# A decode step with a product-key expert layer: index tiles, the sample's gate block, the dot products and the sample's sums take other places

## The chip, the cores and the metric

The kernel runs on one core of a Trainium2 chip. The metric is the time of one execution on the device in microseconds; the times given are medians over several executions. One more execution was recorded by the hardware profiler, and all lines quoted from a profile or a trace come from such an execution. TensorE is PE in the profile (PEld its weight loads), VectorE is DVE, ScalarE is ACT, GpSimd is POOL, SyncE is SP.

## The reference, cut to what matters

The kernel computes one layer of a decoder for 256 prompt tokens and 32 sample tokens (8 sequences of 4). Attention, recurrence, output projection and the first normalisation come first and are not touched. What matters is the expert layer at the end and the normalisation behind it:

```python
def peer_ffn(x, wq, subkeys, u_tab, v_tab):            # x: (B, T, 2048)
    q = (xt @ wq).reshape(n, P_HEADS, 2, P_DKEY // 2)  # 8 heads, two halves of a key
    s = jnp.einsum('nhcd,hckd->nhck', q, subkeys)
    hv, hix = lax.top_k(s, P_TOPK)                     # 16 of 128 in each half
    cand = hv[:, :, 0, :, None] + hv[:, :, 1, None, :]
    cand_e = hix[:, :, 0, :, None] * N_KEYS + hix[:, :, 1, None, :]
    tv, tpos = lax.top_k(cand, P_TOPK)                 # 16 experts per head: 128 per token
    expert = jnp.take_along_axis(cand_e, tpos, axis=-1)
    gate = jax.nn.softmax(tv, axis=-1)
    def block(xb, eb, gb):
        h = jax.nn.gelu(jnp.einsum('cd,chkd->chk', xb, u_tab[eb]), approximate=False)
        return jnp.einsum('chk,chkd->cd', gb * h, v_tab[eb])

x = layer_norm(DEEPNORM_ALPHA * x + peer_ffn(x), ln2_g, ln2_b)
```

There are 128 x 128 = 16384 experts, each with a row of 2048 in `u_tab` and one in `v_tab`, all in float32.

## The kernel before, in words

**The expert layer of the prompt.** The expert number is written as i1 * 128 + i2. For the first 896 columns of x the kernel gathers, for each of the 128 chosen experts of a token, the row piece from a table in HBM and multiplies and sums it on VectorE: a *dot* (`dot`, L1795, one VectorE instruction of 128 tokens x 896 and a read of its sum; `fetch` and `gather`, L455, give it its rows through POOL and a ring `rows` of five buffers). There are 2 x 128 dots, one for each half of the prompt's tokens and each of the 128 choices. For the other 1152 columns it multiplies with every expert on PE: 128 *blocks* (`dense`, L1862 to L1869) of 128 experts each, whose weights come over SP into a ring `ur` of five buffers. The results of the blocks stand in `AW`.

The loop at L1872 writes a block and then one or two dots (`ND`, `NDN`), in seven of eight blocks two. Two dots come before the loop. The 14 dots left behind the loop are written into the first 12 steps of the picking (`NDL`).

**The table.** `table(t)` (L1800) forms for half t of the tokens what the picking reads, transposed: i1, i2, gate and dot of every choice. The two numbers are cut out of the expert number in the tile `ii` (a single buffer, two uses per call), and PE transposes them. `table(0)` is written once eight dots of the second half are done, `table(1)` at step 30.

**The picking.** 64 steps of four tokens each, run as a software pipeline in one loop of 68 (L1973). In a step, `pick` compares all positions with i1 and i2 on VectorE (tile `oo`, L1898), transposes one of them on PE and copies it on ACT; `picked` multiplies it with `AW` on PE (`px`); `product_of` multiplies with the other and sums on VectorE (L1921), adds the dot and takes the Gelu on ACT; `gated` multiplies with the gate; `scaled` scales the comparison on ACT; `put` multiplies both back into `AW` on PE (`pa`) and ACT copies them out.

**The sample's sums.** The 32 sample tokens have their activations already. Their rows of the second table are gathered (`smp_fetch`, two gathers of 512 KB on POOL, into the same ring `rows`) and summed on PE (`smp_add`, tile `fs`, four matmuls with a block `ws` as weights, which spreads each gate over its tokens). 32 such sums stand in steps 14 to 62. `ws` is formed on VectorE ahead of the loop (L1951). Behind the loop the sample's x is added, normalised (`norm_quarters`: statistics on VectorE, one small matmul on PE, a chain of small VectorE instructions, one ACT instruction, two more products) and written out by 16 DMAs on SP (L2013).

**The V stage.** 128 blocks of the second table, three columns groups on PE (L2067) with `AW` as weights, the rows over SP (`rows_load`, L1970), and the last 640 columns by gathers on POOL and sums on VectorE (`row_add`, L2040). The first rows are loaded early into a place of their own; those of the second and third block come in program order behind the sample's outputs on SP.

**What sets the order.** The instructions are written for a planner that puts each engine's queue in order by modelled durations: an instruction that looks ready may move ahead of earlier ones on its engine. Each engine then runs its queue strictly in that order. `pin` (`keep_in_program_order`) holds an instruction behind the one that was written just before it for the same engine. All instructions of the picking are pinned, and the dots inside it too (`keep=True`); the dots of the blocks, `ws`, `table` and the sample's norm are not. `issue_after` holds an instruction behind one that is named. The pools `up`, `dp`, `x4p` and `vp` are stacks on the left side of SBUF: `x4p` (with `ws`) lies where `dp` (with `ur`) was, and `vp` (V stage) lies where `up` and `x4p` were.

Of the kernel before, what the change touches and what calls it, by code (L numbers as in the profile page):

```python
# [12 lines left out]
I32 = mybir.dt.int32  # L13
U32 = mybir.dt.uint32
AF = mybir.ActivationFunctionType
OP = mybir.AluOpType
AX = mybir.AxisListType
PSUM = bass.MemoryType.PSUM
P = 128
# [5 lines left out]
ALPHA = 2.0 ** 0.25  # L25
# [23 lines left out]
NP1 = 8  # L49
NDW = 1  # L50
ND = 1
NDN = 7
NDL = 12
NUR = 5
NRW = 5
NDB = 9
# [94 lines left out]
def hybrid_decode_step(ctx: ExitStack, tc: tile.TileContext, a, outs, dbg=None):  # L151
    nc = tc.nc
    ve, sc, pe, gp, sy = nc.vector, nc.scalar, nc.tensor, nc.gpsimd, nc.sync
# [35 lines left out]
    def bank(tag="pb"):  # L189
        places = [(pool, nm, n) for _, div in psum for t_, pool, nm, n in div for _ in range(n) if t_ == tag]  # L190
        turn[tag] = k = (turn.get(tag, -1) + 1) % len(places)
        pool, nm, n = places[k]
        return pool.tile([P, 512], F32, name=tag, tag=nm, bufs=n)
# [58 lines left out]
    C0, ld = consts(cp, 0)  # L252
# [1536 lines left out]
    def dot(n=1, upto=2 * P, keep=False, ahead=NRW):  # L1789

        for i in range(got[1], min(got[1] + n, upto)):
            t, s_ = dots[i]
            fetch(min(i + ahead, upto))
            r_, h_ = rows_.pop(i), HD[t][:, s_:s_ + 1]
            i_ = ve.scalar_tensor_tensor(r_, r_, 1.0, X1a[t], op0=OP.mult, op1=OP.mult, accum_out=h_)  # L1795
            if keep:
                tc.keep_in_program_order(i_)
            got[1] = i + 1

    def table(t):  # L1800

        pb = bank("pb")
        for q, (op_, v_) in enumerate(((OP.logical_shift_right, 7), (OP.bitwise_and, 127))):
            ii = up([P, P], "ii", I32)
            iff = ii.bitcast(F32)
            ve.tensor_scalar(ii, GI[t], v_, None, op0=op_)
            ve.tensor_copy(iff, ii)
            pe.transpose(pb[:, 128 * q:128 * q + 128], iff, ident)
        pe.transpose(pb[:, 256:384], GE[t], ident)
        pe.transpose(pb[:, 384:], HD[t], ident)  # L1810
        sc.copy(TB[:, :, P * t:P * t + P], pb.rearrange("p (a b) -> p a b", a=4))
# [56 lines left out]
            mm = pe.matmul(ph[:, :NPR], w[:, e, :], Xfd[:, e, :], start=(e == 0), stop=(e == NDB - 1))  # L1868
        return mm, sc.copy(AW[:, i1 // 64, :, i1 % 64], ph[:, :NPR])  # L1869

    tabled = []
    for i1 in range(P):  # L1872
        mm, end = dense(i1)
        n_ = ND + (i1 * NDN % 8 < NDN)
        dot(min(max(P - got[1], 0) or n_, n_))
        if got[1] >= P + 8 and not tabled:
            with tc.issue_after(mm.ins), tc.issue_after(end.ins):
                table(0)
            tabled.append(0)
    kc.close()  # L1880
    dp.close()
    if not tabled:
        dot(P - got[1])
        table(0)
    x4p, vr = Pool("x4", "left"), Pool("vr", "right")
    ig, vh2 = [GI[2], IG], vtab.rearrange("n (q c) -> (n q) c", q=2)
    banks(pt=2, px=2, pa=2, pb=1, fs=1)
# [60 lines left out]

    x4p([P, 4, P], "oT", bufs=2)
    ws = x4p([P, 32, 32], "ws")  # L1950
    ve.tensor_tensor(ws, C0("sum4")[:, None, :32].to_broadcast([P, 32, 32]), GE[2][:, :, None].to_broadcast([P, 32, 32]), OP.mult)  # L1951
    fs, sr = bank("fs"), {}

    def smp_fetch(j):
# [5 lines left out]
    def smp_add(j):  # L1960
        for c in range(4):
            pin(pe.matmul(fs[32 * c:32 * c + 32, :], ws[:, j, :], sr[j, c // 2][:, 512 * (c % 2):512 * (c % 2) + 512],  # L1962
                          start=(j == 0), stop=(j == 31)))

    raw = {}

    def rows_load(k):

        raw[k] = (vp if k % 3 else vr)([P, FD], "v_", bufs=2 if k % 3 else 1)
        return sy.dma_start(raw[k], vtab[P * k:P * k + P, :FD])  # L1970

    left = 2 * P - got[1]
    for s_ in range(68):  # L1973
        if s_ == 30:
            table(1)
        oT = pick(s_) if s_ < 64 else None
        if 3 <= s_ < 66 and s_ % 2:
            gated(s_ // 2 - 1)
        if s_ >= 4:
            put(s_ - 4)  # L1980
        if 0 <= s_ - 3 < 64:
            scaled(s_ - 3)
        if oT is not None:
            picked(s_, oT)
        if 0 <= s_ - 1 < 64:
            product_of(s_ - 1)
        if s_ < NDL:
            dot(-(-left * (s_ + 1) // NDL) + 2 * P - left - got[1], keep=True)
        for j in range(32):
            if s_ == NDL + j * (62 - NDL) // 32:  # L1990
                smp_fetch(j)
        for j in range(32):
            if s_ == NDL + 2 + j * (62 - NDL) // 32:
                smp_add(j)
        if s_ == 46:
            bs_, gs_, x_ = (xa_[:, 512 * n:512 * n + 512] for n in range(3))
            for q in range(4):
                r_, c_ = slice(32 * q, 32 * q + 32), slice(512 * q, 512 * q + 512)
                sy.dma_start(x_[r_, :], X1D[NPR:NT, c_])
                for t_, nm in ((gs_, "ln2_g"), (bs_, "ln2_b")):  # L2000
                    sy.dma_start(t_[r_, :], bass.AP(tensor=a[nm].tensor, offset=a[nm].offset + 512 * q, ap=[[0, 32], [1, 512]]))
        if s_ == 50:
            rows_load(0)
    pb = bank("pb")
    for t in range(2):
        pe.transpose(pb[:, 128 * t:128 * t + 128], TB[:, 2, P * t:P * t + P], ident)
        sc.copy(GE[t], pb[:, 128 * t:128 * t + 128])

    ve.scalar_tensor_tensor(x_, x_, ALPHA, fs, op0=OP.mult, op1=OP.add)
    norm_quarters(x4p, x_, gs_, bs_, "pb")  # L2010
    for q in range(4):
        for i in range(4):
            sy.dma_start(outs[1][:, i, 512 * q:512 * q + 512], x_[32 * q + 8 * i:32 * q + 8 * i + 8, :])  # L2013
    x4p.close()
    up.close()
    banks(pj=2, pb=6)
# [136 lines left out]
```

## Time and profile before

| | |
|---|---|
| median of three executions | 2479.08 us (2474.55 to 2487.72) |
| the profiled execution's own time | 2475.65 us |
| its span in the trace | 2473.9 us |
| PE busy | 2255.7 us (91%) |
| VectorE busy | 1745.4 us (71%) |
| POOL busy | 1336.1 us (54%) |
| expert blocks on PE | 1187.8 to 1685.8 us |
| picking, first to last comparison | 1680.2 to 1916.9 us |
| V stage, first to last matmul | 1931.2 to 2451.4 us |

A line of the trace in order of time reads: start, duration, engine, source line, operation, what it writes and reads, its shape, and in brackets how long its engine stood idle before it and which instruction ended that. In a table of windows a stretch is followed by its length, the busy time of the engines with the number of instructions in brackets, the granted clock of PE, the share of the DMA engines' time in use, and the bytes moved in GB/s.

### The profile page before, as it was taken

The page shows a single profiled execution, that of the slowest core. Times are in us where ns is not written, and L with a number is a line of the kernel's source. Part 1 is how long each engine was busy: PE and PEld are TensorE (multiplying, and loading weights), DVE is VectorE, ACT ScalarE, POOL GpSimd, SP SyncE. Part 2 cuts the span into 40 slices and gives each one's busy share as a digit, 9 for nine tenths or more (in the row PEclk, how much of TensorE's full clock was granted, in tenths as well). Part 3 has the DMA queues.
Part 4 walks back from the last instruction along what each step waited for, and adds up shares of the span by engine and source line. Part 5 has one row for each costly group of instructions (what it writes and reads, how often), then busy time and mean ns, then how long its engine had stood idle before and what let it go on. Part 6 is the DMA issues. An engine that isn't in the chain of part 4 may idle for free.

```text
span 2473.9 us, 42694 instructions
## 1 busy us (share of the span) xinstructions
PE 2255.7 (91%) x15628; PEld 1886.1 (76%) x15628; DVE 1745.4 (71%) x3985; ACT 820.4 (33%) x1591; POOL 1336.1 (54%) x1419
## 2 busy tenths in 40 slices
PE   7979999997988997789999999995899799999996
PEld 7867898885645665578888888884777688888885
DVE  5789766555563446889856545556877799998888
ACT  3433222223341433220111111111777444443443
POOL 5678423233345005578666644655444588886672
PEclk9999999998896996899999999997999899999998
DMA  7777986449478984798699989995666699999994
GB/s 218 229 236 225 284 216 177 119 143 278 171 243 252 316 302 146 288 321 267 213 400 404 398 329 401 383 393 169 181 209 197 242 369 363 363 362 362 345 358 187
DMA packets 327602, 684.09 MB, mean 277 GB/s; under 512 B 82270, under 2 KB 200992, under 8 KB 326464
## 3 DMA queue, kind: packets, MB, share of 16 engines
q1 hardware_dynamic: 246176, 342.58, 41.7%
q0 software_dynamic: 81216, 338.78, 38.2%
q8 instruction: 123, 2.02, 0.3%
q14 instruction: 87, 0.71, 0.1%
HBM read 665.69 MB, written 23.88 MB: 279 GB/s over the span
## 4 chain that ended last, share of the span: by engine, by line
PE 46%; issue 14%; DVE 13%; POOL 11%; DMA 8%; ACT 2%; SPq 1%; POOLq 0%; DVEq 0%; ACTq 0%
PE pb L2067 19%; POOL rows L455 8%; PE pj L424 6%; PE pa L1661 3%; PE px L1910 2%; PE p L1081 2%; DVE sr L1557 2%; PE pa L1943 2%; DMA big<-in_state_rwkv 1%; PE ss L1498 1%; DMA co<-in_cache_cmp_kv,gidx 1%; PE pt L1902 1%; PE fs L1962 1%; DMA rows<-in_peer_u_g,gi 1%; DVE CA L478 1%
## 5 line engine op out<-in xcount | busy, mean ns | idle before, releaser
L1868 PE MATMUL ph<-Xfd,ur 128*128 128x256 f32 x2304 | 497.8, 379 | 0.0
L1868 PEld LDWEIGHTS ph<-Xfd,ur 128*128 128x128 f32 x2304 | 437.4, 190 | 59.5
L455 POOL DMA_INDIRECT rq<-in_peer_v_g,gi x256 | 378.5, 1479 | 142.0 <-DVE fP L2040 86.7
L455 POOL DMA_INDIRECT rows<-in_peer_u_g,gi x256 | 292.5, 1143 | 229.8 <-DVE rows L1795 199.5
L1795 DVE SCALAR_TENSOR_TENSOR rows<-rows,x1a 128x896 f32<-128x896 f32 x256 | 280.2, 1098 | 178.4 <-DMA rows<-in_peer_u_g,gi 178.0
L424 PE MATMUL pj<-XH,wl 128*128 128x288 f32 (+1 forms) x752 | 231.7, 308 | 14.9 <-DVE wl L419 8.5
L424 PE MATMUL pj<-XH,wh 128*128 128x288 f32 (+1 forms) x752 | 229.5, 305 | 15.2 <-DVE ss L754 6.9
L2040 DVE SCALAR_TENSOR_TENSOR fP<-rq,ge,fP 128x640 f32<-128x640 f32 x254 | 223.7, 881 | 5.7 <-DMA rq<-in_peer_v_g,gi 3.3
L424 PE MATMUL pj<-XL,wh 128*128 128x288 f32 (+1 forms) x752 | 225.9, 301 | 0.0
L2067 PE MATMUL pb<-vl,ah 128*128 128x512 f32 (+1 forms) x768 | 207.6, 378 | 1.3 <-DVE vl L2060 0.5
L1869 ACT COPY AW<-ph 128x256 f32<-128x256 f32 x128 | 77.2, 610 | 396.6 <-PE ph L1868 391.5
L2067 PE MATMUL pb<-vh,ah 128*128 128x512 f32 (+1 forms) x768 | 188.0, 380 | 22.1 <-ACT vh L2059 22.1
L2067 PE MATMUL pb<-vh,al 128*128 128x512 f32 (+1 forms) x768 | 205.8, 376 | 0.0
L417 ACT CAST wh<-wraw 128x512 fp32r<-128x512 f32 (+1 forms) x188 | 114.8, 616 | 228.9 <-PE pj L424 175.6
L2067 PEld LDWEIGHTS pb<-vh,ah 128*128 128x128 f32 x768 | 145.5, 196 | 44.9 <-ACT vh L2059 25.7
L478 DVE SCALAR_TENSOR_TENSOR CA<-co,wbc,CA 128x256 f32<-128x256 f32 x248 | 133.4, 575 | 48.7 <-DMA co<-in_cache_cmp_kv,gidx 48.7
L424 PEld LDWEIGHTS pj<-XH,wl 128*128 128x128 f32 (+1 forms) x752 | 143.8, 191 | 26.8 <-DVE wl L419 12.5
L2067 PEld LDWEIGHTS pb<-vl,ah 128*128 128x128 f32 x768 | 144.9, 195 | 24.2 <-DVE vl L2060 5.1
L424 PEld LDWEIGHTS pj<-XH,wh 128*128 128x128 f32 (+1 forms) x752 | 144.1, 192 | 21.4 <-DVE ss L754 7.3
L2067 PEld LDWEIGHTS pb<-vh,al 128*128 128x128 f32 x768 | 145.3, 195 | 19.4
L424 PEld LDWEIGHTS pj<-XL,wh 128*128 128x128 f32 (+1 forms) x752 | 144.2, 192 | 1.5 <-issue 1.2
L419 DVE TENSOR_TENSOR wl<-wraw,wh 128x512 fp32r<-128x512 f32 (+1 forms) x141 | 101.8, 731 | 44.4 <-ACT wh L417 43.8
(844 smaller groups left out, 4339.2 us busy)
## 6 DMA issues: line engine op xcount, KB each, us to landing
ur<-in_peer_u_t SPq DMA_DIRECT2D x128, 576.0 KB
wraw<-in_w_in SPq DMA_DIRECT2D x152, 256.0 KB
cw<-in_w_out SPq DMA_DIRECT2D x32, 512.0 KB
wraw<-in_w_out SPq DMA_DIRECT2D x32, 512.0 KB
wraw<-in_peer_wq SPq DMA_DIRECT2D x32, 512.0 KB
cw<-in_peer_wq SPq DMA_DIRECT2D x32, 512.0 KB
wraw<-in_w_in SPq DMA_DIRECT2D x64, 128.0 KB
co<-in_state_win_kv SPq DMA_DIRECT2D x16, 512.0 KB
```

Of the source, the lines that this page charges most:

```text
L417: sc.copy(wh[:, :, :n], w[:, :, :n])
L419: i_ = en.tensor_tensor(wl[:, :, :n], w[:, :, :n], wh[:, :, :n].bitcast(F32), OP.subtract)
L424: last[2] = pe.matmul(pb[:n, :nt], wi[:, k, :n], xi[(o + k) // 8][:, (o + k) % 8, :nt], start=(o + k == 0 and wi is wh and xi is xh), stop ...
L455: gp.indirect_dma_start(out=dst, out_offset=None, in_=rows_, in_offset=bass.IndirectOffsetOnAxis(ap=ix, axis=0))
L478: ve.scalar_tensor_tensor(d_, x_, w_, d_, op0=OP.mult, op1=OP.add)
L1081: pe.matmul(pb[hs[c], 64 * m:64 * m + 64], lhs(hs[c], m), rhs(hs[c], m), start=True, stop=True)
L1661: pe.matmul(acc[t], xi[:, e, P * t:P * t + P], wi[:, e, :], start=(k == e == n_ == 0), stop=(k == 6 and e == 1 and n_ == 2))
L1795: i_ = ve.scalar_tensor_tensor(r_, r_, 1.0, X1a[t], op0=OP.mult, op1=OP.mult, accum_out=h_)
L1868: mm = pe.matmul(ph[:, :NPR], w[:, e, :], Xfd[:, e, :], start=(e == 0), stop=(e == NDB - 1))
L1869: return mm, sc.copy(AW[:, i1 // 64, :, i1 % 64], ph[:, :NPR])
L2040: ve.scalar_tensor_tensor(fP[t], r_, w_, fP[t], op0=OP.mult, op1=OP.add)
L2067: pe.matmul(acc[3 * t + q][:, :n_], wi[:, P * t:P * t + P], xi[:, 512 * q:512 * q + n_], start=(k == 0 and wi is ah and xi is vh), stop=(k ...
```

## The change

1. The index tile `ii` has four buffers, one for each use.
2. `ws` is formed in step 1 of the picking, and pinned there.
3. `NDN` is 8: every block is followed by two dots, so that all 256 are written by the end of the blocks. The dots inside the picking go, and `NDL` with them. `table(0)` is written when 24 dots of the second half are done, `table(1)` at step 20.
4. The sample's 32 sums stand in steps 3 to 58, each sum two steps behind its gathers as before.
5. The sample's last addition, norm and outputs are a function `sample_out`, called at step 60 of the loop. The loads of x and of the norm's weight and bias that it needs move from step 46 to step 24.

What is computed stays the same.

```diff
-NDN = 7
-NDL = 12
+NDN = 8
...
-            ii = up([P, P], "ii", I32)
+            ii = up([P, P], "ii", I32, bufs=4)
...
-    tabled = []
     for i1 in range(P):
         mm, end = dense(i1)
         n_ = ND + (i1 * NDN % 8 < NDN)
         dot(min(max(P - got[1], 0) or n_, n_))
-        if got[1] >= P + 8 and not tabled:
+        if got[1] == P + 24:
             with tc.issue_after(mm.ins), tc.issue_after(end.ins):
                 table(0)
-            tabled.append(0)
...
-    if not tabled:
-        dot(P - got[1])
-        table(0)
...
-    ve.tensor_tensor(ws, C0("sum4")[:, None, :32].to_broadcast([P, 32, 32]), GE[2][:, :, None].to_broadcast([P, 32, 32]), OP.mult)
...
+    def sample_out():
+
+        ve.scalar_tensor_tensor(x_, x_, ALPHA, fs, op0=OP.mult, op1=OP.add)
+        norm_quarters(x4p, x_, gs_, bs_, "pb")
+        for q in range(4):
+            for i in range(4):
+                sy.dma_start(outs[1][:, i, 512 * q:512 * q + 512], x_[32 * q + 8 * i:32 * q + 8 * i + 8, :])
+
...
-    left = 2 * P - got[1]
+    dot(2 * P - got[1])
+    at = lambda j: 2 + 55 * j // 31
+    bs_, gs_, x_ = (xa_[:, 512 * n:512 * n + 512] for n in range(3))
     for s_ in range(68):
-        if s_ == 30:
+        if s_ == 20:
             table(1)
...
-        if s_ < NDL:
-            dot(-(-left * (s_ + 1) // NDL) + 2 * P - left - got[1], keep=True)
+        if s_ == 1:
+            pin(ve.tensor_tensor(ws, C0("sum4")[:, None, :32].to_broadcast([P, 32, 32]),
+                                 GE[2][:, :, None].to_broadcast([P, 32, 32]), OP.mult))
         for j in range(32):
-            if s_ == NDL + j * (62 - NDL) // 32:
+            if s_ == at(j) - 1:
                 smp_fetch(j)
         for j in range(32):
-            if s_ == NDL + 2 + j * (62 - NDL) // 32:
+            if s_ == at(j) + 1:
                 smp_add(j)
-        if s_ == 46:
-            bs_, gs_, x_ = (xa_[:, 512 * n:512 * n + 512] for n in range(3))
+        if s_ == 24:
...
+        if s_ == 60:
+            sample_out()
...
-    ve.scalar_tensor_tensor(x_, x_, ALPHA, fs, op0=OP.mult, op1=OP.add)
-    norm_quarters(x4p, x_, gs_, bs_, "pb")
-    for q in range(4):
-        for i in range(4):
-            sy.dma_start(outs[1][:, i, 512 * q:512 * q + 512], x_[32 * q + 8 * i:32 * q + 8 * i + 8, :])
```

## The prediction

> **What bounds the kernel now.** I read the stages first (busy time per engine in chosen windows), then VectorE's instructions in order of time, then the queues. Columns of the windows: stretch, length, then PE, PEld, DVE, ACT, POOL busy (instructions), granted clock, DMA share, GB/s.
>
> ```profile
> 1300.00:1450.00 150.00, 150.00 (x697) 132.05 (x696) 88.97 (x162) 23.82 (x39) 91.81 (x81) 1.00 1.01 399
> 1450.00:1500.00 50.00, 50.00 (x235) 43.92 (x234) 18.99 (x39) 8.26 (x14) 19.64 (x18) 1.00 0.86 311
> 1500.00:1660.00 160.00, 160.00 (x743) 140.85 (x742) 93.47 (x170) 25.00 (x41) 92.44 (x85) 1.00 1.01 398
> 1686.00:1712.00 26.00, 1.93 (x14) 1.26 (x11) 19.12 (x37) 0.96 (x2) 19.99 (x16) 0.63 0.74 247
> 1712.00:1757.00 45.00, 31.25 (x208) 28.29 (x209) 42.30 (x147) 23.22 (x62) 23.42 (x16) 0.83 0.58 175
> 1757.00:1916.00 159.00, 156.24 (x1256) 121.65 (x1254) 122.11 (x502) 118.82 (x328) 72.41 (x59) 1.00 0.64 201
> 1927.00:1950.00 23.00, 11.87 (x36) 9.81 (x37) 8.83 (x17) 6.85 (x8) 8.60 (x8) 0.70 0.52 183
> 2000.00:2200.00 200.00, 200.00 (x939) 176.54 (x938) 186.37 (x185) 88.22 (x78) 167.70 (x107) 1.00 0.97 363
> ```
>
> The expert blocks (up to 1686) and the V stage are full on PE, and no instruction of theirs changes. The picking from 1757 on is full on PE too. The holes lie between: 26 us with 2 us of matmul (1686 to 1712), 45 us with 31 (the first picking steps), 23 us with 12 (between picking and V stage). The change works on these three. VectorE in order of time says why the first is there:
>
> ```profile
> 1467.93 0.23 DVE L1806 TENSOR_SCALAR ii<-gi 128x128 int32<-128x128 int32 x1 [16.49 <-PE pb L1808]
> 1472.86 0.23 DVE L1806 TENSOR_SCALAR ii<-gi 128x128 int32<-128x128 int32 x1 [2.42 <-PE pb L1808]
> ...
> 1678.06 1.23 DVE L1951 TENSOR_TENSOR ws<-CT,ge 128x1024 f32<-128x1024 f32 x1 [18.17 <-PE ph L1868]
> ...
> 1680.21 1.22 DVE L1898 TENSOR_TENSOR oo<-CT,TB 128x1024 f32<-128x1024 f32 x1
> 1685.93 0.23 DVE L1806 TENSOR_SCALAR ii<-gi 128x128 int32<-128x128 int32 x1 [4.50 <-PE pb L1808]
> ...
> 1712.44 1.22 DVE L1898 TENSOR_TENSOR oo<-CT,TB 128x1024 f32<-128x1024 f32 x1
> 1715.85 1.22 DVE L1898 TENSOR_TENSOR oo<-CT,TB 128x1024 f32<-128x1024 f32 x1
> ...
> 1754.48 1.22 DVE L1898 TENSOR_TENSOR oo<-CT,TB 128x1024 f32<-128x1024 f32 x1
> ...
> 1915.65 1.22 DVE L1898 TENSOR_TENSOR oo<-CT,TB 128x1024 f32<-128x1024 f32 x1
> 1917.90 0.69 DVE L2009 SCALAR_TENSOR_TENSOR x1a<-x1a,fs 128x512 f32<-128x512 f32 x1 [1.03 <-PE fs L1962]
> ...
> 1930.08 0.69 DVE L1457 TENSOR_TENSOR x1a<-x1a 128x512 f32<-128x512 f32 x1
> ```
>
> The dot products (L1795) stand still for 16.49 + 2.42 us in the middle of the blocks, for 18.17 us ahead of the gate block, and for 4.50 us more. Each time an instruction that waits for PE stands in front of them: an index tile with a single buffer, or the gate block, whose place in SBUF a weight buffer still holds. So the backlog of dots runs after the last block, and the second step of the picking (1712.44) stands behind it.
>
> **Edits 1 to 3: index tiles, gate block, two dots per block.** Dots alone, per window (busy us, rows; two rows are one dot), then the gathers that feed them, first and last of 14:
>
> ```profile
> 1450.00:1500.00 50.00, 18.25 (x35) 1.00 0.86 311
> ...
> 1600.00:1660.00 60.00, 35.78 (x66) 1.00 1.02 407
> 1660.00:1712.00 52.00, 20.08 (x37) 0.81 0.56 194
> 1712.00:1760.00 48.00, 14.62 (x28) 0.84 0.60 179
> ```
> ```profile
> 1691.47 0.95 POOL L455 DMA_INDIRECT rows<-in_peer_u_g,gi  x1 [0.30 <-DVE rows L1795]
> ...
> 1710.82 1.43 POOL L455 DMA_INDIRECT rows<-in_peer_u_g,gi  x1 [0.30 <-issue]
> ```
> ```profile
> 1643.08 23.64 SPq L1865 DMA_DIRECT2D ur<-in_peer_u_t  x7
> ```
>
> While the DMA engines are full (share 1.01), dots run at their pace: 33 in 60 us, or 0.55 per us; I take 0.535, as the stretch 1500 to 1660 has 85 gathers. How many a block is given in the program does not set this pace; a ring of five buffers does. So "two per block" slows no block: weights and dots already share full engines and PE is busy 150 of 150 us. What it does is to take the last 14 dots out of the picking.
>
> In 1450 to 1500 there are 17.5 dots where 27 would fit, so the single index buffer cost 9.5 dots. At 1660 there are (37 + 28)/2 = 32.5 left; without that wait 23. The gate block no longer stands in front; now the first instruction of the picking is pinned behind the last dot, so nothing that waits for PE can stand before a dot. From 1660 to about 1671 (the last weights are issued by 1666.7) 11 x 0.535 = 6 dots go, and 17 are left. After that a gather takes (1710.82 - 1691.47)/13 = 1.49 us, so 25 us: the last dot ends at about **1696.5**, 11 us after the last block, not at 1712. Bounds: 1691, if from 1666.7 on a gather leaves every 0.95 + 0.30 us (the first of the 14); 1710, if the pace of the full stretch (60/33 = 1.82 us) holds to the end, 1702, and the last gather's landing of 7.4 us (below) is not hidden.
>
> Then the picking starts from nothing. From a comparison to its product's end the trace has 5.15 us at the low clock (1712.44 to 1715.51 + 2.08, rows below). A step's four products with their sums take 1.1 (3.41 between the comparisons at 1712.44 and 1715.85, less 1.22 and a dot of 1.09, the 35.78 us of the 33 above). With the gate block's 1.23 that makes 7.6 us, so the third comparison comes at 1704.1. Before it came at 1715.85. **Gain 11.7 us.** Queued behind the gate block is that comparison, which the 7.6 hold already; its readers on PE come only at step 3.
>
> **Edit 4: sums over steps 2 to 58.** What a step costs with and without four sums (fs), from PE in order of time:
>
> ```profile
> 1713.72 1.11 PE L1902 MATMUL pt<-CT,oo 128*128 128x128 f32 x4 [24.91 <-DVE oo L1898]
> 1715.51 2.08 PE L1910 MATMUL px<-AW,oT 128*128 128x128 f32 x8 [0.68 <-ACT oT L1904]
> ...
> 1908.20 0.63 PE L1902 MATMUL pt<-CT,oo 128*128 128x128 f32 x4
> ...
> 1909.56 1.16 PE L1910 MATMUL px<-AW,oT 128*128 128x128 f32 x8
> 1910.65 1.07 PE L1962 MATMUL fs<-rows,ws 128*32 128x512 f32 x8
> 1911.65 0.66 PE L1902 MATMUL pt<-CT,oo 128*128 128x128 f32 x4
> ...
> 1914.31 0.63 PE L1902 MATMUL pt<-CT,oo 128*128 128x128 f32 x4
> ...
> 1944.01 2.72 PE L2067 MATMUL pb<-vh,ah 128*128 128x512 f32 x6 [6.96 <-ACT vh L2059]
> ```
>
> A step with sums takes 3.45 us (1908.20 to 1911.65), one without 2.66. Check: the 51 steps from 1754.48 to 1915.65 hold all 32 sums, 32 x 3.45 + 19 x 2.66 = 160.9; the trace has 161.2. After the change six sums move to the ten steps from the third comparison on: 6 x 3.45 + 4 x 2.66 = 31.3, and about 3 for the low clock at the start (the product took 2.08 instead of 1.16). Before, these ten took 38.6 with their dots. **Gain 4.3.** The other 51 steps keep 26 sums: 156.2. **Gain 5.0.** The earlier gathers (two per sum, POOL) come behind the last dot's in POOL's queue and have three steps until they are read. The twelve small loads of x, weights and bias move from step 46 to 24, but what they overwrite is read by the dots, so they wait on SP for those at either place, and nothing is due behind them before the outputs. The table of the second half (step 20, not 30) needs the last dot too, long done by then. These cost nothing; if the dots ran to step 30, the table would hold step 32.
>
> **Edit 5: the sample's norm and its outputs inside the loop.** Its two parts go opposite ways. Pins hold order on VectorE, PE and ACT: the comparison of step 61 now stands behind the norm's last product. The norm's chain ran from 1917.90 to 1930.77 among the last steps. Lower bound nothing, if all of it slips into idle spots of steps 59 and 60; upper bound the 12.9 us whole. Of these 2.2 were products of the last two steps in between, the first 1.9 or so can run before step 60 ends, as fs is complete at step 58, and PE has a step of 2.66 in hand: I take **6 lost**. The last steps lose L2009 (0.69) and a statistics instruction over the same 512 values from their own way: **gain 1.5**.
>
> A hole in PE has an after-effect here: after 6.96 us idle, six matmuls of the V stage took 2.72 us. [...]
>
> What the outputs held up, SP and POOL in order of time:
>
> ```profile
> 1930.80 6.42 SPq L2013 DMA_DIRECT2D out<-x1a  x16
> 1937.90 0.36 SPq L1970 DMA_DIRECT2D v__18333<-in_peer_v  x1
> ```
> ```profile
> 1939.27 0.96 POOL L455 DMA_INDIRECT rq<-in_peer_v_g,gi  x1 [29.87 <-DMA out<-x1a]
> ```
>
> The V stage's second and third loads stand on SP behind 16 outputs, these behind the norm; the gathers wait for the outputs too. After the change the outputs leave about step 61, so the loads can land under the last steps. What can be won is PE's idle time of 1927 to 1950, 23 - 11.87 = 11.1 us, of which 6.96 is the one hole. The gathers also come some 11 us earlier: they stood until 1939.27, and can now start when the last step has let go of its tables, about 1927 on the old clock. Bounds: 7 (the hole alone) and 14 (the low clock of 0.70 over 11.87 us gone as well). **Gain 11**: the V stage later lives at a DMA share of 0.97 and cannot start faster than its gathers.
>
> **Sum.** 11.7 + 4.3 + 5.0 + 1.5 - 6 + 11 = 27.5 us off this execution's own 2475.65 (span 2473.9 and 1.75 around it): 2448.2. The median shown, 2479.08, lies 3.4 above this execution; I add 1.5 for that: **2450**.
>
> **Rivals.** (a) *Dots end late*, 1708: full engines give them no more. The start gains nothing: 16 us in all, 2461. Against: 1500 to 1660 ran at the full pace for 160 us. (b) *Norm costs its 12.9 us, V stage gains only 7*: 16 us in all, 2461. For: ACT and PE are in the chain. (c) *Better*: dots end at 1691 and the norm hides: 39 us, 2438. (d) *The change doesn't do what it says*: some other instruction planned too early holds the dots, as the order comes from planned durations; the hole stays, and only 11.5 remain (5.0 + 1.5 - 6 + 11): 2465. (e) *Slower*: the sample's gathers bind the picking. The five buffers hold 2.5 sums; a gather lands in
>
> ```profile
> DMA to landing us min/median/max: 4.2/7.4/9.6
> ```
>
> so a sum needs (7.4 + 1.4 + 1.1)/2.5 = 4 us (1.43 issue, 1.07 to be read), and one comes every 1.75 steps, 5.4 us (174 us for steps 3 to 58: 32 x 3.45 + 24 x 2.66). It binds from a landing of 11 us and eats the whole gain from 13. At 15 us 32 sums take 224 us, 50 more: 2500. Against: the longest landing is 9.6. (f) *Slower*: the blocks move only what the V stage does, 363 GB/s, with two dots per block.
>
> ```profile
> L1868 PE MATMUL ph<-Xfd,ur 128*128 128x256 f32 x2304 | 497.8, 379 | 0.0
> ...
> ur<-in_peer_u_t SPq DMA_DIRECT2D x128, 576.0 KB
> ```
>
> Weights take 152 GB/s of it (576 KB in 497.8/128 = 3.89 us), dots 211, or 0.46 per us (128 x 896 words each). Done at 1450 are 256 - 17.5 - 85 - 32.5 = 121; the last would end at 1746, and the third comparison 38 us later than before. The rest gives 16 back: 2499. [...] The windows disagree: 398 and 399 GB/s over 310 us.
>
> **How the numbers follow.** Chances: forecast 0.55, (a) 0.15, (b) 0.08, (c) 0.10, (d) 0.07, (e) 0.03, (f) 0.02. 0.5% is 12.4 us, which this measurement can just tell from no change: below 2466.7 is faster. The forecast, (c) and three quarters of (a) and (b) are faster, 0.82; most of (d) and the rest of (a), (b) are the same, 0.12; (e), (f) and a little of (d) are slower, 0.06. The range takes (a) to (d): 2437 to 2467, a microsecond wider at either end.
>
> **What would show it.** No PE wait in front of L1806 in the blocks; no dot after 1700 and none between comparisons; the second comparison 1 to 5 us after the last dot; the 51 last steps at 156 plus one step of 8 to 10 us at step 61; outputs on SP ahead of the last steps' end and no gap in PE at the V stage's second block. Wrong, if a dot still runs at 1710, if fs waits for gathers, or if the V stage's PE is idle for another reason.

## The result, and the profile after

The changed kernel takes **2451.45 us** (median of four executions, 2450.20 to 2464.38), the kernel before beside it on the same chip 2476.82. The ratio is 0.989, with a 95% interval of 0.986 to 0.993. On another chip, with five executions against seventeen, it was 0.987 (0.984 to 0.989). The profiled execution took 2451.44 us, with a span of 2449.7. So the kernel is faster by about 1.1%, and the predicted 2450 lies 1.5 us from the median. The parts of the sum do not all lie so near.

The stages ahead of the blocks, which the change leaves alone, end between 1184.7 and 1207.9 us in the profiles below. Profiles are therefore compared from the first weight load of the blocks (1187.8 before, 1184.7 after) to the end of the span: 1286.1 us before, 1265.0 after, 21.1 less.

The windows of the kernel after, as in the prediction (stretch, length, then PE, PEld, DVE, ACT, POOL busy with instructions, granted clock, DMA share, GB/s):

```profile
1210.00:1220.00 10.00, 9.53 (x45) 8.07 (x44) 9.96 (x30) 4.09 (x9) 7.84 (x13) 1.00 0.01 2
1450.00:1500.00 50.00, 50.00 (x235) 43.99 (x234) 28.59 (x52) 8.37 (x14) 28.84 (x27) 1.00 1.01 390
1600.00:1660.00 60.00, 60.00 (x280) 52.82 (x279) 36.10 (x65) 9.15 (x15) 42.33 (x33) 1.00 1.01 398
...
1686.00:1712.00 26.00, 19.04 (x88) 15.83 (x87) 18.42 (x43) 4.25 (x8) 14.38 (x11) 0.80 0.80 245
1712.00:1757.00 45.00, 43.73 (x351) 34.31 (x350) 34.69 (x144) 33.24 (x92) 19.96 (x16) 1.00 0.59 177
...
1915.00:1930.00 15.00, 13.34 (x51) 11.52 (x52) 11.77 (x12) 6.82 (x7) 12.24 (x10) 0.77 0.88 312
```

The rows stand at fixed times, not at fixed steps. The first stretch holds 19.04 us of matmul where it held 1.93, but 10 of these belong to the blocks, which end at 1696.0 in this kernel. Counted from the end of the blocks to the third comparison, the first hole shrank from 30.1 to 11.8 us. Of the second stretch PE is busy 43.73 of 45 us, and the third is gone as a hole: PE is busy 13.34 of 15 us between picking and V stage. The stretch 1450 to 1500, where the dots stood still, now runs at the full DMA share. One row is new: from 1210 to 1220, early in the blocks, next to nothing is moved (2 GB/s).

VectorE of the kernel after in order of time, with the index tiles first (a row of the view of that tile: count, then first and last start):

```profile
L1805 DVE TENSOR_SCALAR ii<-gi x4: 215/224/272, 1222.7 to 1224.3; 128x128 int32<-128x128 int32 x4
```
```profile
1699.10 1.11 DVE L1794 SCALAR_TENSOR_TENSOR rows<-rows,x1a 128x896 f32<-128x896 f32 x1
...
1700.14 2.35 DVE L1892 TENSOR_TENSOR oo<-CT,TB 128x1024 f32<-128x1024 f32 x2
...
1706.60 1.22 DVE L1991 TENSOR_TENSOR ws<-CT,ge 128x1024 f32<-128x1024 f32 x1
...
1707.73 1.22 DVE L1892 TENSOR_TENSOR oo<-CT,TB 128x1024 f32<-128x1024 f32 x1
...
1738.42 1.22 DVE L1892 TENSOR_TENSOR oo<-CT,TB 128x1024 f32<-128x1024 f32 x1
...
1877.67 1.22 DVE L1892 TENSOR_TENSOR oo<-CT,TB 128x1024 f32<-128x1024 f32 x1
...
1881.07 1.22 DVE L1892 TENSOR_TENSOR oo<-CT,TB 128x1024 f32<-128x1024 f32 x1
...
1883.78 1.22 DVE L1892 TENSOR_TENSOR oo<-CT,TB 128x1024 f32<-128x1024 f32 x1
1886.02 0.69 DVE L1960 SCALAR_TENSOR_TENSOR x1a<-x1a,fs 128x512 f32<-128x512 f32 x1 [1.03 <-PE fs L1955]
...
1888.38 1.22 DVE L1892 TENSOR_TENSOR oo<-CT,TB 128x1024 f32<-128x1024 f32 x1
...
1896.08 0.69 DVE L1456 TENSOR_TENSOR x1a<-x1a 128x512 f32<-128x512 f32 x1
1896.69 1.22 DVE L1892 TENSOR_TENSOR oo<-CT,TB 128x1024 f32<-128x1024 f32 x1
...
1903.66 1.22 DVE L1892 TENSOR_TENSOR oo<-CT,TB 128x1024 f32<-128x1024 f32 x1
```

All four index tiles are filled at 1223 us, as soon as the expert numbers are there, and no dot waits behind one. The last dot ends at 1700.2 and the first two comparisons follow at once. The 13th comparison is at 1738.42, the 61st at 1888.38, the 64th at 1903.66. The norm stands between 1886 and 1896.7.

What was not foreseen lies at the start of the blocks. The waits of SP's queue in 1180 to 1235, then SP, POOL and PE in order of time:

```profile
SPq L1971 <- POOL gi L1418: 19.1, 1, 19.1
```
```profile
1188.94 15.87 SPq L1864 DMA_DIRECT2D ur<-in_peer_u_t  x5
1224.00 0.33 SPq L1971 DMA_DIRECT2D v__17742<-in_peer_v  x1
1224.43 2.77 SPq L1864 DMA_DIRECT2D ur<-in_peer_u_t  x5
```
```profile
1223.77 0.21 POOL L1418 CAST gi<-EF 128x16 int32<-128x16 f32 x1
```
```profile
1234.27 28.08 PE L1867 MATMUL ph<-Xfd,ur 128*128 128x256 f32 x117 [9.66 <-DMA ur<-in_peer_u_t]
```

The load of the V stage's first rows (L1971) stands on SP between the tenth and the eleventh load of the blocks' weights. It waits 19.1 us until POOL has read the last `EF`, a small tile of the top-k stage, and the weights queue behind it. PE then stands still for 9.66 us. The blocks last 511 us (1184.9 to 1696.0) instead of 498. In the second profile of the changed kernel (after_2 below) the load waits 22.4 us and PE 6.9.

The end of the picking and the start of the V stage on PE, SP and POOL; the last fence is of the kernel before, for the comparison:

```profile
1898.06 1.08 PE L1896 MATMUL pt<-CT,oo 128*128 128x128 f32 x4 [5.56 <-DVE TB L1923]
1898.93 1.92 PE L1937 MATMUL pa<-oo 128*128 128x128 f32 x8
1900.64 1.56 PE L1904 MATMUL px<-AW,oT 128*128 128x128 f32 x8
...
1916.66 2.71 PE L2066 MATMUL pb<-vh,ah 128*128 128x512 f32 x6 [2.47 <-ACT ah L2055]
...
1926.95 1.44 PE L2066 MATMUL pb<-vh,ah 128*128 128x512 f32 x6
```
```profile
1896.80 5.36 SPq L1964 DMA_DIRECT2D out<-x1a  x16
1902.85 0.36 SPq L1971 DMA_DIRECT2D v__18333<-in_peer_v  x1
```
```profile
1913.75 0.96 POOL L454 DMA_INDIRECT rq<-in_peer_v_g,gi  x1 [38.81 <-PE pa L1937]
```
```profile
1950.10 1.44 PE L2067 MATMUL pb<-vh,ah 128*128 128x512 f32 x6
```

The outputs leave before the last steps are done, and the two loads behind them at 1902.85 and later; V's second block meets no wait. From the 64th comparison to the first matmul of V's third block it took 34.45 us before (1915.65 to 1950.10) and takes 23.29 now.

Where the 21.1 us went, against the prediction's terms:

| stretch | before | after | gained | foreseen |
|---|---|---|---|---|
| first weight load to third comparison | 528.0 | 523.0 | 5.0 | 11.7 |
| third to 13th comparison | 38.6 | 30.7 | 7.9 | 4.3 |
| 13th to 61st | 152.4 | 150.0 | 2.4 | -1.0 with the next row |
| 61st to 64th | 8.8 | 15.3 | -6.5 | |
| 64th to V's third block | 34.5 | 23.3 | 11.2 | 12.5 |
| V's third block to the end | 523.8 | 522.8 | 1.0 | 0 |

The other 3.1 us of this pair of profiles lie ahead of the blocks.

### The profile page after: what moved, and what is told of

Same layout as the page of the kernel before. It is cut to its first block, busy times and chain, and to the rows that moved or that the text cites. A ratio compares the mean times of both kernels' runs of the same rounds, so it can differ in the third digit from the quotient of the medians.

```text
span 2449.7 us, 42718 instructions
## 1 busy us (share of the span) xinstructions
PE 2254.7 (92%) x15628; PEld 1886.4 (77%) x15628; DVE 1748.2 (71%) x3985; ACT 819.9 (33%) x1591; POOL 1332.6 (54%) x1419
## 4 chain that ended last, share of the span: by engine, by line
PE 51%; issue 13%; DVE 12%; POOL 11%; DMA 9%; ACT 2%; SPq 1%; POOLq 0%; DVEq 0%; ACTq 0%
PE pb L2066 20%; POOL rows L454 9%; PE pj L423 8%; PE pa L1660 3%; PE px L1904 3%; PE pa L1937 2%; DVE sr L1556 2%; PE p L1080 2%; PE pt L1896 2%; DMA co<-in_cache_cmp_kv,gidx 2%; PE ss L1497 1%; DMA rows<-in_peer_u_g,gi 1%; PE fs L1955 1%; DVE CA L477 1%; DMA co<-in_cache_sel_kv,sidx 1%
## 5 line engine op out<-in xcount | busy, mean ns | idle before, releaser
L423 PEld LDWEIGHTS pj<-XH,wl 128*128 128x128 f32 (+1 forms) x752 | 144.4, 192 | 22.4 <-DVE wl L418 9.1
```

The lines of the kernel that those rows point to most:

```text
L423: last[2] = pe.matmul(pb[:n, :nt], wi[:, k, :n], xi[(o + k) // 8][:, (o + k) % 8, :nt], start=(o + k == 0 and wi is wh and xi is xh), stop ...
```

## The experiments

Two questions stood at the start. Why does the load of V's first rows wait? One answer is **space**: three more index tiles make the left stack of SBUF 1.5 KB per partition larger (128 int32 each), it then shares places with V's first rows, and their load must wait for what was there. `EF` belongs to a pool that lies above `up` on the same stack, so it would be moved with it. Another is the **order of work**: the eighth dot in every eighth block, or the index tiles that are filled early. And is each edit worth what its step of the prediction says, or do the edits need each other?

All results in one table. "To 64th" is from the first weight load of the blocks to the 64th comparison, "rest" from there to the end of the span, both from the profile. The ratio is to the kernel before on the same chip.

| kernel | median us | ratio, 95% interval | to 64th | rest | sum |
|---|---|---|---|---|---|
| before | 2476.82 | 1 | 727.8 | 558.3 | 1286.1 |
| after | 2451.45 | 0.989 (0.986, 0.993) | 719.0 | 546.0 | 1265.0 |
| after_2 | 2461.93 | 0.987 (0.984, 0.989) | 721.2 | 546.3 | 1267.5 |
| pad_before | 2494.91 | 1.007 (1.005, 1.010) | 745.5 | 557.8 | 1303.3 |
| load_pinned | 2447.53 | 0.985 (0.981, 0.989) | 713.7 | 545.0 | 1258.7 |
| load_pinned_2 | 2462.65 | 0.988 (0.985, 0.990) | 714.3 | 545.2 | 1259.5 |
| ii_one | 2485.69 | 1.004 (1.001, 1.006) | 758.7 | 545.1 | 1303.8 |
| ws_front | 2494.91 | 1.006 (1.004, 1.008) | 760.8 | 545.0 | 1305.8 |
| dots_in_pick | 2466.62 | 0.994 (0.991, 0.997) | 737.7 | 546.3 | 1284.0 |
| sums_late | 2473.04 | 0.992 (0.990, 0.995) | 721.7 | 546.4 | 1268.1 |
| dots_late_sums | 2476.78 | 0.995 (0.993, 0.997) | 727.3 | 545.1 | 1272.4 |
| norm_behind | 2457.76 | 0.989 (0.984, 0.993) | 715.0 | 557.8 | 1272.8 |
| spread | 2449.78 | 0.985 (0.981, 0.989) | 712.8 | 545.1 | 1257.9 |

### Space: pad_before and load_pinned

pad_before is the kernel before with an unused tile of the size of three index tiles:

```diff
     TB = up([P, 4, NPR], "TB")
+    up([P, 3 * P], "pad")
```

> The kernel before, with a tile of 384 words per partition that nobody uses added to the stack 'up': the space of three index buffers, and nothing else. Theory 1 (the space alone moves the load of the first V rows to a place where it waits): the load leaves SP at about 1224 instead of 1188, PE waits about 10 us for weights early in the blocks, the blocks end 8 to 13 us later; the time is 2481 to 2490, 4 to 13 us more than before, as part of the delay goes into the backlog of dots that sets the picking's start. Rival (the space does nothing, the wait comes from the dots): 2477, and no wait for ur.

SP's waits and PE of pad_before:

```profile
SPq L1971 <- POOL gi L1419: 19.3, 1, 19.3
```
```profile
1235.86 14.39 PE L1869 MATMUL ph<-Xfd,ur 128*128 128x256 f32 x56 [10.55 <-DMA ur<-in_peer_u_t]
```

Space alone, with no other edit, gives the same wait for the same reader of `EF`, and 17.2 us more to the end (1303.3 against 1286.1). The medians lie 15.5 apart (2494.91 against 2479.41 of the kernel before on that chip); 4 to 13 was expected. In the kernel before the same load left at 1188.1, after a wait of its own of 15.5 us for a matmul, and PE met no wait for `ur`.

load_pinned is the changed kernel with that load held at its place in the program, step 50 of the picking:

```diff
         if s_ == 50:
-            rows_load(0)
+            pin(rows_load(0))
```

> The changed kernel, with the load of the V stage's first rows (rows_load(0)) pinned behind the SP instruction written before it. In the changed kernel that load stood on SP from 1205 to 1224 us for POOL and held the expert weights behind it; PE then waited 9.7 us for weights. Theory 1 (a neighbour in SBUF: the three more index buffers push the left stack under the place of that load, so that it must wait for POOL, and the weights queue behind it on SP): the weights come as before, the blocks last about 498 us again, no PE wait for ur; the last dot ends at 1693 to 1697; 4 to 8 us less than the changed kernel, 2443 to 2447. Rival (two dots per block load the DMA engines so that weights come late): the wait for ur stays at about 10 us and the time at 2451.

> The load of V's first rows pinned at step 50. Theory: no PE wait for ur; from the first weight load to the end 1258 to 1260 us, the median 5 to 7 us under the changed kernel's beside it. Rival: the earlier difference was the spread between executions; the two medians lie within 3 us.

The load no longer stands among the first weights on SP, no wait for `ur` is left in either profile, and the stretch to the end is 6.3 us shorter than that of after (another chip) and 8.0 shorter than that of after_2 (the same chip). The blocks shorten more, to 501.9 and 499.7 us from 511.2 and 514.4, but the dots then end 4.8 and 10.0 us behind them and hold the picking. The first comparison, which follows the last dot, comes 506.6 and 509.6 us after the first weight load, against 515.4 and 514.1. So the wait is shown to come from space (that `EF` and V's rows share a place is inferred from it), and to cost the changed kernel 6 to 8 us in profiles. The timed medians do not show it: on the first chip the ratio was lower than the changed kernel's on its own chip (0.985 against 0.989), side by side the two medians lie 0.7 us apart, where 5 to 7 less were expected. Executions of one kernel lie 10 to 25 us apart there.

The order of work falls as an answer: load_pinned keeps two dots in every block and all early index tiles, and pad_before has neither.

### One index tile again: ii_one

```diff
-            ii = up([P, P], "ii", I32, bufs=4)
+            ii = up([P, P], "ii", I32)
```

> The changed kernel with one index buffer again (edit 1 undone alone). By the prediction's step the index waits come back (16.5 and 2.4 us in front of the dots, some 9.5 dots of 1.5 us each behind the last block), which costs 10 to 14 us at the start of the picking; by theory 1 the 10 us wait for weights goes at the same time, so the blocks end about 13 us earlier: together 2450 to 2458, with the last dot at 1700 to 1708 and the last block at 1683 to 1686. Rival (the wait for weights does not hang on the space): the last block stays at 1696 and the time goes to 2460 to 2466.

VectorE of ii_one in order of time, then its dots alone in two windows (busy us, rows, clock, DMA share, GB/s):

```profile
1487.28 0.23 DVE L1805 TENSOR_SCALAR ii<-gi 128x128 int32<-128x128 int32 x1 [19.39 <-PE pb L1807]
...
1693.63 0.23 DVE L1805 TENSOR_SCALAR ii<-gi 128x128 int32<-128x128 int32 x1 [26.86 <-PE pb L1807]
```
```profile
1660.00:1700.00 40.00, 9.80 (x19) 0.96 0.44 171
1700.00:1745.00 45.00, 28.42 (x52) 0.50 0.84 277
```

The wait for `ur` is gone (the load is back at its old place), and the sum still is 38.8 us longer. The expected 2450 to 2458 was far off: the median is 2485.69. Besides the wait in the middle of the blocks, the last index tile of the second table is planned in front of the last dots and holds them for 26.86 us until the blocks are done. With no comparison allowed ahead of the last dot, the 31 dots that are left run alone (26 of them from 1700 on), and the first comparison comes at 1742.8. The kernel before also had 31 left at the end of its blocks, but 14 of them ran among the first steps of the picking.

### The gate block in front again: ws_front

```diff
     ws = x4p([P, 32, 32], "ws")
+    ve.tensor_tensor(ws, C0("sum4")[:, None, :32].to_broadcast([P, 32, 32]), GE[2][:, :, None].to_broadcast([P, 32, 32]), OP.mult)
...
-        if s_ == 1:
-            pin(ve.tensor_tensor(ws, C0("sum4")[:, None, :32].to_broadcast([P, 32, 32]),
-                                 GE[2][:, :, None].to_broadcast([P, 32, 32]), OP.mult))
```

> The changed kernel with the gate block formed ahead of the loop again, not pinned (edit 2 undone alone). Compared from the first weight load of the blocks to the end of the trace, as the stages ahead of it vary by 15 us between executions: before 1286.1, changed 1265.0. Theory (an instruction that waits for PE and may move ahead stands in front of dots): the gate block, and with it the first comparisons pinned behind it, stand in front of some 25 dots again; VectorE idles 20 to 30 us at the end of the blocks, and these dots run among the first steps of the picking, 1.1 us each in steps of 3: 10 to 25 us more, 1275 to 1290. Rival (the index waits alone made the backlog, the gate block only showed it): no dot after the last block by more than 4 us, 1265.

VectorE of ws_front, its dots alone, and PE at the first sum:

```profile
1692.16 1.22 DVE L1945 TENSOR_TENSOR ws<-CT,ge 128x1024 f32<-128x1024 f32 x1 [49.80 <-PE ph L1867]
```
```profile
1660.00:1700.00 40.00, 0.00 (x0) 1.00 0.27 91
1700.00:1760.00 60.00, 35.69 (x66) 0.57 0.80 263
```
```profile
1753.67 1.92 PE L1956 MATMUL fs<-rows,ws 128*32 128x512 f32 x4 [22.25 <-DMA rows<-in_peer_v,gi]
```

The gate block, unpinned, is planned 50 us too early and stops VectorE until its place is free. Not one dot runs from 1660 to 1700; 33 run behind the blocks, among the comparisons, with PE at a granted clock of 0.57. Within this time PE waits 22.25 us for the rows of the first sum, whose gathers stand behind those of the dots on POOL, and 18.9 us for two comparisons. The price is 40.8 us; 10 to 25 were expected. How much of it would be left with later sums no run shows.

### Dots in the picking, and later sums: dots_in_pick, sums_late, dots_late_sums

dots_in_pick takes back edit 3, sums_late the early sums of edit 4 in the changed kernel, dots_late_sums both. The first diff is of dots_in_pick, the second of sums_late; dots_late_sums has the two:

```diff
-NDN = 8
+NDN = 7
+NDL = 12
...
-    dot(2 * P - got[1])
+    left = 2 * P - got[1]
...
+        if s_ < NDL:
+            dot(-(-left * (s_ + 1) // NDL) + 2 * P - left - got[1], keep=True)
```
```diff
-    at = lambda j: 2 + 55 * j // 31
+    at = lambda j: 13 + 44 * j // 31
```

> The changed kernel with 14 dots in the first 12 steps of the picking again (edit 3 undone alone; the earlier sums stay, so these steps now hold six sums too). From the first weight load to the end: changed 1265.0. By the prediction the 14 dots cost VectorE 1.1 us each on the steps' path, as before: the start comes some 4 us earlier, as the last dot is then no longer what the picking waits for, and the steps lose 8 to 15: 1269 to 1276. Rival (in steps that PE bounds, with a sum of 1.0 us, the dots hide): 1261 to 1264, and edit 3 was no gain.

> The changed kernel with the sample's 32 sums over steps 13 to 58 in place of 2 to 58. Theory: PE is full from the third comparison on, so a sum costs its 0.8 us wherever it stands: third to 13th comparison about 27 us in place of 30.7, the steps behind it some 4 to 5 us longer, from the first weight load to the end 1264 to 1267 us. Rival: the first steps wait for something else than PE, so early sums are free there; third to 13th comparison stays at 30 and the whole loses 4 to 6 us (1269 to 1271).

> The kernel dots_in_pick (14 dots in the first twelve steps) with the sample's sums over steps 13 to 58. Theory: in dots_in_pick the sums waited 9.0 us for their gathers, which stood behind the dots' gathers; without sums in these steps that wait and the low clock behind it go: 1271 to 1276 us from the first weight load to the end, in place of 1284. Rival: the dots themselves hold the first steps, with sums or without: 1281 or more.

PE's waits from 1700 to 1770 in dots_in_pick (total us, times, longest):

```profile
PE fs L1958 <- DMA rows<-in_peer_v,gi: 6.9, 3, 2.8
...
PE fs L1958 <- DMA rows<-in_peer_v,ig: 2.1, 2, 1.8
```

With dots and sums in the same steps the sums wait 9.0 us for their gathers, which share POOL and the ring `rows` with the dots' gathers. Later sums take these waits away and the sum falls by 11.6, from 1284.0 to 1272.4, as expected. So edit 3 costs 19.0 when taken back beside early sums (1284.0 against 1265.0), more than was expected, and 4.3 beside late ones (1272.4 against 1268.1).

PE of sums_late in order of time, transposes (`pt`, one per step) and sums (`fs`):

```profile
1735.38 0.63 PE L1896 MATMUL pt<-CT,oo 128*128 128x128 f32 x4 [1.02 <-DVE oo L1892]
...
1741.49 0.63 PE L1896 MATMUL pt<-CT,oo 128*128 128x128 f32 x4 [1.01 <-DVE oo L1892]
...
1757.16 0.66 PE L1896 MATMUL pt<-CT,oo 128*128 128x128 f32 x4
1759.64 1.06 PE L1955 MATMUL fs<-rows,ws 128*32 128x512 f32 x8
1760.63 0.66 PE L1896 MATMUL pt<-CT,oo 128*128 128x128 f32 x4
1763.11 1.06 PE L1955 MATMUL fs<-rows,ws 128*32 128x512 f32 x8
1764.10 0.66 PE L1896 MATMUL pt<-CT,oo 128*128 128x128 f32 x4
1766.77 0.63 PE L1896 MATMUL pt<-CT,oo 128*128 128x128 f32 x4
```

Two steps without a sum take 6.11 us (1735.38 to 1741.49), for PE waits 1.0 us for a comparison in every second one. Two steps with one sum take 6.14 (1760.63 to 1766.77), two with two sums 6.94 (1757.16 to 1764.10). The first sum of a pair of steps is free; only the second costs its 0.8. The kernels before and after repeat these durations through most of the picking. Spread wider, fewer pairs hold two. My theory for sums_late was wrong: its first ten steps took 32.6 us without any sum, not 27, against 30.7 and 34.2 in the two profiles of the changed kernel with six. Its later steps lost 6.3 (13th to 61st: 156.3 against 150.0). The rival holds for the steps. The whole gave 1268.1, as sums_late's last dot came earlier than the changed kernel's, so that the first comparison was at 508.1. The timed median lies 11.1 above the changed kernel's beside it, which the profiles show only to 0.6 to 3.1. The profiled execution of sums_late was the shortest of its six (2466.23), that of after_2 the longest of its five (2473.94); where the rest lies is open.

### The norm behind the loop: norm_behind; cut in pieces: spread

```diff
-        if s_ == 60:
-            sample_out()
...
+    sample_out()
```

> The changed kernel with the sample's norm and outputs behind the loop again (edit 5 undone alone; sums stay at steps 3 to 58). By the prediction's steps edit 5 is worth 11 + 1.5 - 6 = 6.5 us, so 2458. By the rows of the changed kernel it costs 8.4 us at steps 59 to 61 and brings 10.4 + 0.8 behind the loop, so only 3: 2454. A rival is that the planner lets the norm slip forward from there too, so that nothing changes: 2451.

PE of norm_behind at the start of the V stage, SP's outputs, and one instruction of the norm's statistics on VectorE:

```profile
1938.98 2.72 PE L2065 MATMUL pb<-vh,ah 128*128 128x512 f32 x6 [7.81 <-ACT vh L2057]
```
```profile
1925.28 6.93 SPq L1964 DMA_DIRECT2D out<-x1a  x16
```
```profile
1903.38 0.15 DVE L1447 TENSOR_TENSOR smv<-smv,ssq 128x1 f32<-128x1 f32 x1
```

The hole of the kernel before at V's second block is back, 7.81 us wide. The outputs stand on SP 14.4 us behind the 64th comparison (1910.9), in the changed kernel 6.9 us ahead of it. From the first to the 64th comparison norm_behind takes 196.6 us, 6.9 less than the changed kernel; behind it 11.7 more. The first comparison comes 3.0 later in this profile. That is 11.7 - 6.9 = 4.8 for edit 5, and 7.8 with the difference that has nothing to do with it; the prediction had 6.5. But the run takes the edit back only in part. The norm is not pinned, and its first part, the addition and the statistics up to L1447, still stands inside the loop: 1903.38 is ahead of the 62nd comparison, as 1889.52 is in the changed kernel. The price of that part is in both kernels. The times can't tell the two apart.

spread is load_pinned with the norm written in eleven pieces, one per step from step 51, the sums over steps 2 to 49 and the last two products on POOL:

```diff
-    at = lambda j: 2 + 55 * j // 31
+    at = lambda j: 2 + 47 * j // 31
+    tail = sample_out()
...
-        if s_ == 60:
-            sample_out()
+        if s_ >= 51:
+            for _ in take(tail, 1):
+                pass
```

> The changed kernel with the pinned load of load_pinned, and with the sample's norm cut into eleven pieces, one at the end of each step from 51 on, so that no comparison stands behind the whole chain; the sums end at step 50 for that, and the two last products of the norm run on POOL. load_pinned took 1258.7 from the first weight load to the end, and lost 8.4 us in steps 59 to 61 as the changed kernel did. Theory (the loss is waiting: VectorE for PE and ACT inside the chain, PE for VectorE behind it): the steps from 51 on last 2.7 to 3.2 us each with no gap of PE above 1 us, 4 to 6 us less: 1252 to 1255, the median 2438 to 2444. Rival (the loss is VectorE's own work of 5.6 us, which has to run in these steps either way): 1257 to 1259.

The same 28 us window, of the changed kernel and of spread:

```profile
1876.00:1904.00 28.00, 20.88 (x158) 18.13 (x158) 21.51 (x94) 17.36 (x47) 0.00 (x0) 0.88 0.11 28
```
```profile
1876.00:1904.00 28.00, 24.32 (x195) 22.45 (x194) 24.92 (x114) 23.72 (x66) 2.93 (x2) 1.00 0.20 63
```

PE's hole and the low clock behind it are gone, and first to 64th comparison takes 201.8 us where load_pinned took 207.1 and 204.7. The sum is 0.8 below the better load_pinned, since its last dot ended later (first comparison at 511.0). That is what the rival gave. No version is shown to beat the changed kernel in time.

## Why the prediction was right, point by point

**Edits 1 to 3.** Right in kind: no wait for PE stands before a dot, about 24 dots run behind 1660 (25 at the same distance from the first weight load; foreseen 23), and the third comparison comes 7.6 us after the last dot, as foreseen (the terms as written add up to 7.5). Rivals (a) and (d) fall. The term was 11.7 and came out at 5.0. What failed is the step from "no instruction of theirs changes" to blocks that last as long as before. The edit of the index tiles moved a load, and the blocks became 13 us longer. The last dot was foreseen 508.7 us after the first weight load (1696.5 less 1187.8); the first comparison, which follows it at once, came 515.4 after it with the wait, and 506.6, 509.6 and 511.0 in the three profiles without it (load_pinned, load_pinned_2, spread). Their third comparisons come 13.8, 10.8 and 9.4 us earlier than before, around the 11.7. So the working of the dots' pace holds and what was left out is a resource: the place of the tile.

**That these edits are three.** The prediction gave them one answer together; taking back one costs 38.8, 40.8 or 19.0 us, while all five gain 21.1. A wait that is left alone costs more than its own step, for the dots that it holds are no longer planned among the steps of the picking: they run behind the blocks by themselves (ii_one), or among steps that have sums to carry (9.0 us of waits in dots_in_pick, 22.25 in ws_front).

**Edit 4.** The two terms came out at 7.9 and at 3.6 without the norm, against 4.3 and 5.0. The 3.6 are the 2.4 of the table and 1.2 that the norm's first part took of that stretch: the step from 1883.78 to 1888.38 took 4.60, the last one at the same turn (1877.67 to 1881.07) 3.40. The step that failed is the price of a sum: "3.45 with, 2.66 without" mixed it up with the turn of the steps, which alternate without sums too. That the check over 51 steps came out at 160.9 against 161.2 was chance. The first ten steps took 30.7 and 34.2 us in two profiles of one kernel, so 3 us of that 7.9 are spread.

**Edit 5.** The norm cost 7.7 (1.2 and 6.5), where I took 6 within bounds of 0 and 12.9. norm_behind, which moves only the second part, gives 6.9 for that. PE stood 5.56 us, and eight `pa` behind it took 1.92 us where eight take 1.06; from 1895 to 1902 the granted clock was 0.52. With the four `pt` ahead of them (1.08 against 0.63) and the eight `px` behind them (1.56 against 1.16) that is 1.7 us more, for which the 6 held nothing; 8 would have been the better figure. The V stage's start and the last steps together gave 11.2, foreseen 12.5: outputs ahead of the last steps' end, no gap at V's second block.

**The rivals on DMA.** (f) falls: with two dots per block the windows 1450 to 1500 and 1600 to 1660 moved 390 and 398 GB/s, not 363, with PE busy all the time. (e) did not happen in the changed kernel, where PE never waited for a sum's gathers; dots_in_pick (9.0 us) and ws_front (22.25 us) show it, once dots' gathers stood in front.

**The sum.** 27.5 was foreseen and 24.2 measured in the pair of profiles, 21.1 of it from the blocks on. Foreseen too high were the start of the picking (by 6.7, the wait for the load), the later steps (by 1.4), the norm (by 1.7) and the V stage's start (by 1.3). Foreseen too low were the first ten steps (by 3.6), and not foreseen at all 1.0 in the V stage and 3.1 ahead of the blocks, which the change does not touch. These cancel in part, so the median is right partly by luck.

## What to carry to other kernels

A tile's buffers cost space even where their instructions cost nothing (in pad_before the space alone cost 17.2 us from the blocks to the end): after such an edit, see in the DMA queue's own order what each early load waits for, and who is queued behind it. Where several waits hold one queue, take all of them away together: here each one left in cost more than the whole change brings or nearly so (19.0 for edit 3, of which later sums leave 4.3). A unit price is safe only if the steps with and without the unit are compared at the same turn of a loop that alternates.

## What the runs showed of the hardware that was not expected

A load that waited on SP held the loads behind it: 19.1 us of waiting for one tile emptied the DMA engines for 10 us (2 GB/s) and stopped PE for 9.66 us (changed kernel; 6.9 in its second profile) and 10.55 (pad_before), although the ring of weights has five buffers.

The granted clock stayed low where PE had little to do: 0.57 over 60 us of which PE was busy 16.1 in short groups of matmuls (ws_front), 0.50 over 45 us of which it was busy 1.3 (ii_one).

The stages ahead of the blocks, which no edit is meant to touch, differed by 23 us between profiles (1184.7 to 1207.9). A gain of 6 to 8 us behind them is seen in four profiles and not in medians of four to six executions.
